# Expert weights loaded in rows of 8 KB instead of 4 KB, one expert to a piece

## The chip, the cores and the metric

The kernel runs on one core of a Trainium2 chip. The metric is the device time of one execution in microseconds (us), the median of several runs. Instructions run on five engines, each with its own queue: TensorE (PE) for matrix products, whose weight loads (PEld) are shown apart; VectorE (DVE); ScalarE (ACT); GpSimd (POOL); and SyncE (SP), which here only issues DMA transfers. The transfers of a core share 16 DMA engines.

## The reference

One encoder layer over 256 tokens of width 1024 in float32. Two mixing branches (stick-breaking attention and retention) are gated, added and projected; after that comes a mixture of experts, which is the stage that this case is about:

```python
def hierarchical_moe(xn, ...):               # xn: 256 tokens x 1024
    group_probs = softmax(xt @ w_group_router + b_group_router)
    p_group, g_sel = top_k(group_probs, 1)                  # 1 of 4 groups
    top_vals, top_idx = top_k(in_group_expert_logits, 2)    # 2 of its 4 experts
    gate = softmax(top_vals) * p_group
    ...
    for e in range(16):
        hidden = silu(xt @ w_exp_gate[e]) * (xt @ w_exp_up[e])   # 1024 -> 512
        y = y + combine[:, e:e + 1] * (hidden @ w_exp_down[e])   # 512 -> 1024
```

The result is added to the layer's stream and normed once more. The weights of the 16 experts are 16 x 3 x 2 MiB = 96 MiB, and every one of them is read.

## The kernel before

**Stages.** The input projections, the two branches and the output projection come first and are not touched. Their weights also come as DMA transfers of 1 MiB, with rows of 1 KB or 2 KB, and one table, `dec`, comes with rows of 8 KB. Then the router picks the experts of each token, and the experts are worked through in eight pairs, `i` = 0 to 7, each expert with up to 64 token places.

**The work on a pair on PE.** `gather` brings the tokens of four pairs to their places with one-hot matrices (32 products of 128x256, line 945, ahead of pair 0 between the first pieces of its gate, and again ahead of pair 4). Its result `xgt` is the stationary operand of `proj` (line 996), which runs once for gate and once for up: eight blocks `c` of 128 input features, each for both experts `j`. The matrix `hn` (the normed stream) is the stationary operand of the gather's products, read through `features(c2, c)`, which says which 128 input features make block `c`: it has to be the set of rows that the weight tile holds at that place. `hidden` (line 1016) transposes the pair's hidden values in four blocks of 128; `down` (line 1032) multiplies them with the down weights; `scatter` (line 1050) adds the pair's result to the tokens. The order on PE for a pair is gate, down of the pair before, up; in the tail it is up of pair 7, down of pair 6, down of pair 7.

**The loads.** All weights go through 25 slots of 8 KB a partition (1 MiB each). `plan` puts the loads down in the order in which they are used: g0, u0, g1, d0, u1, g2, d1, u2, g3, d2, u3, d3, g4, u4, then g, d, u of pairs 5 and 6, then g7, u7, d6, d7 (g, u and d are gate, up and down, each four pieces of 1 MiB, written here g0.0 to g0.3). `pump` (line 163 issues) hands out loads as long as the list of free slots has one; the list is first in, first out. A piece's slot goes back to the list in `after`, which `proj` and `down` call behind the products of a piece, and SP waits in the program for those products before it issues the load that takes the slot. The SP queue is in order: a load that waits holds back all behind it. The transfers of SP count on eight semaphores in turn (DMAHW0 to DMAHW7), so each also waits until the eighth before it has landed.

**A piece before.** For gate and up, piece `r` has features 256r to 256r+255 of both experts of the pair, two consecutive rows of 512 floats to a partition, in two transfers of 512 KB, one for each expert. A down piece has 256 rows of one expert in one transfer, as two rows of 1024 floats a partition that are 128 rows apart. Either way a contiguous run is 4 KB. The work slot, which holds the hidden values and the one-hot matrices of a pair, is taken in `after` when u0.0 is dropped.

Of the kernel before, what the change touches and what calls it, by code (L numbers as in the profile page):

```python
# [17 lines left out]
P = 128  # L18
T = 256
D = 1024  # L20
# [62 lines left out]
def pack(ins):  # L83
    w = np.concatenate([ins["w_group_router"][0], ins["w_expert_router"][0]], axis=1)
    b = np.concatenate([ins["b_group_router"][0], ins["b_expert_router"][0]])
    return np.ascontiguousarray(np.concatenate([
        ins["norm_mix_g"][0].reshape(KC, P).T,
        ins["b_gate"][0].reshape(16, P).T,
        ins["ret_norm_g"][0].reshape(8, P).T,
        ins["norm_ffn_g"][0].reshape(8, P).T,  # L90
        np.broadcast_to(b[None, :], (P, 20)),
        w.reshape(KC, P, 20).transpose(1, 0, 2).reshape(P, 160),
        ins["norm_final_g"].reshape(8, P).T,
        ins["norm_ffn_g"][0].reshape(4, P, 2).transpose(1, 0, 2).reshape(P, 8),
    ], axis=1))


# [1 line left out]
def layer(ctx: ExitStack, tc, cst, dec, prm, x, w_in, w_gate, w_sb_out, w_ret_out,  # L99
          w_out, w_exp_gate, w_exp_up, w_exp_down, out):  # L100
    nc = tc.nc
    pe, act, dve, pool, sp = nc.tensor, nc.scalar, nc.vector, nc.gpsimd, nc.sync
# [17 lines left out]
    def take(shape=(P, 2048), dt=F32):  # L120
        s = free.pop(0)
        uid[0] += 1
        t = big.tile(list(shape), dt, name=f"b{uid[0]}", tag=f"s{s}")
        held[id(t)] = (s, t)
        return t
# [5 lines left out]
    def small(shape, dt=F32, name=None, bufs=1, tag=None):  # L131
        uid[0] += 1
        return sm.tile(list(shape), dt, name=f"{name}_{uid[0]}", tag=tag or name, bufs=bufs)

    def bank(name="d", dt=F32):
        uid[0] += 1
        return pp[name].tile([P, 512 if dt == F32 else 1024], dt, name=f"p{uid[0]}", tag=name)
# [7 lines left out]
    raws = {}  # L145
# [5 lines left out]
    def rows(w, r0, nk, c0, n):  # L151
        return w[r0:r0 + nk * P, c0:c0 + n].rearrange("(kc p) n -> p kc n", p=P)

    def plan(key, shape, parts, hook=None):
        loads.append((key, shape, parts, hook))

    def pump():
        while loads and loaded[0] < limit[0] and free:
            key, shape, parts, hook = loads.pop(0)
            t = raws[key] = take(shape)  # L160
            loaded[0] += 1
            for i, (at, src) in enumerate(parts):
                sp.dma_start(t[at], src)
                if hook:
                    hook(i)
# [6 lines left out]
    def drop(key):  # L172
        give(raws.pop(key))
# [19 lines left out]
    ident = cw[:, 2048 - P:2048]  # L193
# [4 lines left out]
    ident = identr.bitcast(F32)  # L198
# [259 lines left out]

    def plan_rows(which, w, i):
        for r in range(4):  # L460
            e = [w[0, 2 * i + j][256 * r:256 * r + 256].rearrange("(p k) n -> p k n", k=2) for j in range(2)]
            plan((which, i, r), [P, 2, 2, 512], [((slice(None), j), e[j]) for j in range(2)])

    def plan_down(i):
        for r in range(4):
            e = rows(w_exp_down[0, 2 * i + r // 2], 256 * (r % 2), 2, 0, D)
            cut = (i, r) == (NP - 1, 3)
            plan(("d", i, r), [P, 2, D],
                 [((slice(None), k), e[:, k]) for k in range(2)] if cut else [(slice(None), e)])
# [11 lines left out]
    for which, i in STEPS:  # L481
        if which == "d":
            plan_down(i)
        else:
            plan_rows(which, w_exp_gate if which == "g" else w_exp_up, i)
# [3 lines left out]
    key, shape, parts, hook = loads[2]  # L489
# [253 lines left out]
    i = 0  # L743
# [138 lines left out]
    xgt = take([P, KC, T])  # L882
# [50 lines left out]
    y2, work, gs = [], {}, {}  # L933

    def features(c2, c):
        return slice(256 * c2 + c, 256 * c2 + 256, 2)

    def gather(k, pt, cs=range(4)):

        for c2 in cs:  # L940
            ps = bank("m").rearrange("p (c s) -> p c s", c=2)
            for tb in range(NB):
                for h in range(2):
                    for c in range(2):
                        pe.matmul(ps[:, c, :], hn[h][:, tb, features(c2, c)], pt[tb].rearrange("p e s -> p (e s)"),  # L945
                                  start=c == 0 and tb == 0 and h == 0, stop=c == 1 and tb == 1 and h == 1,
                                  skip_group_check=True)
            tt(xgt[:, 2 * c2:2 * c2 + 2, :], ps,
               fp[:, 2 * c2:2 * c2 + 2][:, :, None].to_broadcast([P, 2, 2 * P]), op=ALU.mult)
# [23 lines left out]

    def after(key):
        drop(key)
        if not work and key == ("u", 0, 0):
            w = take([P, 2048])
            work.update(b=w[:, 0:512], ht=[w[:, 512 + 512 * k:1024 + 512 * k].rearrange("p (f s) -> p f s", f=4)
                                           for k in range(2)],
                        pb=w[:, 1536:1664].bitcast(BF16), S=[small([P, T], F32R, "S")])  # L980
        if not y2 and key == ("u", 0, 3):
            w = take([P, 2048], F32R)
            y2.append(w[:, 0:1024].rearrange("p (h n) -> p h n", h=2))
            work["S"].append(w[:, 1024:1024 + T])
        pump()

    def proj(i, which, ps, hook):
        o = 64 * (i % 4)
        for r in range(4):
            if hook:  # L990
                hook(r)
            w = raws[(which, i, r)]
            for k in range(2):
                c = 2 * r + k
                for j in range(2):
                    pe.matmul(ps[64 * j:64 * j + 64, :], xgt[:, c, o:o + 64], w[:, j, k, :],  # L996
                              start=c == 0, stop=c == KC - 1)
            after((which, i, r))

    def gate(i, hook=None):  # L1000
        g = bank("g")
        proj(i, "g", g, hook)
        return g
# [4 lines left out]
    def up(i, hook=None):  # L1008
        u = bank("g")
        proj(i, "u", u, hook)  # L1010
        stt(work["b"], u, gs[i][:, 0:1], work["b"], op0=ALU.mult, op1=ALU.mult)  # L1011

    def hidden(i):
        hps = bank("m").rearrange("p (f s) -> p f s", f=4)
        for f in range(4):
            pe.transpose(hps[:, f, :], work["b"][:, f * P:(f + 1) * P], ident)  # L1016
        act.activation(work["ht"][i % 2], hps, AF.Copy)  # L1017

    def down(i, hook=None):

        ht = work["ht"][i % 2]
        ys = [(bank(b), cs) for b, cs in zip("gm", pieces(i))]
        for r in range(4):
            if hook:
                hook(r)
            w = raws[("d", i, r)]
            j = r // 2
            for y, cs in ys:
                for k in range(2):
                    f = 2 * (r % 2) + k  # L1030
                    for q in range(2):
                        pe.matmul(y[64 * q:64 * q + 64, cs], ht[:, f, 64 * j:64 * j + 64],  # L1032
                                  w[:, k, 512 * q + cs.start:512 * q + cs.stop],
                                  start=r == 0 and k == 0, stop=r == 3 and k == 1)
            after(("d", i, r))
        for y, cs in ys:
            hilo(y2[0][:, 0, cs], y2[0][:, 1, cs], y[:, cs])
# [56 lines left out]
    def head(first):  # L1094
# [21 lines left out]
        for i in range(1, NP):  # L1116
            def in_gate(r):
                if r == 2:
                    tables(i)
                    if i != 4:  # L1120
                        hidden(i - 1)

            def in_up(r):
                if r == 2 and i < NP - 1:
                    scatter(i - 1)
                if r == 2 and i == NP - 1:
                    for q in range(2):
                        final_gain(q)

            if i == 4:  # L1130
                pt = [onehot(1, tb, rank[:, tb, :]) for tb in range(NB)]
                gather(1, pt, [0, 1])
                hidden(3)
                gather(1, pt, [2, 3])
                down(3)
            places(i)
            g = gate(i, in_gate)
            silu(i, g)
            if first and i == 2:
                most.append(nc.values_load(cnt[0:1, 0:1], min_val=0, max_val=T))  # L1140
            if i != 4 and i < NP - 1:
                down(i - 1)
            up(i, in_up)

    def tail():
        i = NP - 1

        def in_first(r):
            if r == 2:
                hidden(i)  # L1150

        def in_second(r):
            if r == 1:
                scatter(i - 1)

        down(i - 1, in_first)
        down(i, in_second)
# [83 lines left out]
```

## Time and profile before

| what | value |
|---|---|
| median of 3 runs | 463.96 us (463.85 to 464.1) |
| profiled execution, its own time | 464.75 us |
| its span, first to last instruction | 463.0 us |
| mean granted TensorE clock | 0.994 |
| PE busy | 443.4 us (96%) |
| DMA | 142.49 MB, mean 308 GB/s |

Shares of busy time are means over the whole span. PE is shown busy nearly throughout, yet a matrix product that waits for its operand can count as busy, so the chain of waits and the DMA rate in each stretch say more. The chain that ended last goes over PE for 80% of the span and over DMA for 14%, all of the latter behind 385 us but for the first microseconds.

### The profile page before, as it was taken

To read this page: it belongs to the slowest core of one execution; us is meant where nothing else is said; L and a number is where in the kernel's file an instruction comes from. 1 tells how busy PE (TensorE), PEld (TensorE's weight loads), DVE (VectorE), ACT (ScalarE), POOL (GpSimd) and SP (SyncE) were. 2 spreads that over 40 slices of the span, in tenths; PEclk is the share of its full clock that TensorE was granted. 3 is DMA by queue.
4 is the path that set the end of the run, shared out by engine and by line. 5 is a ranking of instruction groups with operands and counts; after the bars stand their busy time and mean duration, and the time that the engine had idled before them with its cause. 6 is when DMAs were issued, how large, how long until landed. Compare 5 with 4: busy or idle time off the path is not lost.

```text
span 463.0 us, 6743 instructions
## 1 busy us (share of the span) xinstructions
PE 443.4 (96%) x2715; PEld 298.8 (65%) x2715; DVE 186.9 (40%) x349; ACT 166.7 (36%) x246; POOL 22.2 (5%) x36
## 2 busy tenths in 40 slices
PE   7999999999999999999999999999989999999881
PEld 6699878888899999999996333333353333333240
DVE  4756487654457865578538410101031001010003
ACT  3643688895653655444543020101000010102003
POOL 2400110110002200000001000000000000000000
PEclk9999999999999999999999999999999999999997
DMA  8999975249302279995949999999999999999972
GB/s 282 353 382 392 388 250 172 90 121 316 107 1 92 92 237 372 408 398 183 368 159 335 346 370 390 410 408 411 408 409 410 409 410 409 409 408 409 410 288 97
DMA packets 58037, 142.49 MB, mean 308 GB/s; under 512 B 3344, under 2 KB 23952, under 8 KB 57872
## 3 DMA queue, kind: packets, MB, share of 16 engines
q1 hardware_dynamic: 57568, 141.35, 81.2%
q10 hardware_dynamic: 432, 0.65, 0.5%
q8 instruction: 23, 0.38, 0.3%
q14 instruction: 14, 0.11, 0.1%
HBM read 140.93 MB, written 1.05 MB: 307 GB/s over the span
## 4 chain that ended last, share of the span: by engine, by line
PE 80%; DMA 14%; DVE 2%; ACT 1%; issue 1%; POOL 1%; SPq 0%; ACTq 0%; DVEq 0%
PE p L294 20%; PE p L996 17%; PE p L1032 8%; PE p L281 8%; PE p L284 7%; PE p L282 7%; DMA b<-in_w_exp_down 6%; DMA b<-in_w_exp_up 5%; DMA b<-in_w_exp_gate 2%; PE p L945 2%; PE z L586 1%; PE p L1050 1%; DMA b<-in_x 1%; PE p L688 1%; PE p L629 1%
## 5 line engine op out<-in xcount | busy, mean ns | idle before, releaser
L253 DVE TENSOR_TENSOR b<-b,b 128x1024 fp32r<-128x1024 f32 x72 | 88.7, 1241 | 71.7 <-ACT b L251 70.6
L996 PE MATMUL p<-b,b 128*64 128x512 f32 x512 | 117.1, 597 | 0.2 <-DMA b<-in_w_exp_up 0.2
L294 PE MATMUL p<-b,b 128*128 128x512 f32 (+1 forms) x504 | 102.7, 359 | 0.5 <-ACT b L251 0.3
L251 ACT ACTIVATE b<-b 128x1024 fp32r<-128x1024 f32 x72 | 75.5, 1056 | 76.6 <-PE p L282 47.7
L294 PEld LDWEIGHTS p<-b,b 128*128 128x128 f32 x504 | 82.6, 190 | 14.6 <-ACT b L251 0.7
L996 PEld LDWEIGHTS p<-b,b 128*64 128x64 f32 x512 | 35.8, 137 | 68.1 <-issue 64.4
L281 PE MATMUL p<-b,b 128*128 128x256 f32 x288 | 71.6, 286 | 0.0
L282 PE MATMUL p<-b,b 128*128 128x256 f32 x288 | 70.7, 283 | 0.0
L1032 PE MATMUL p<-b,b 128*64 128x512 f32 (+1 forms) x288 | 57.8, 548 | 2.7 <-DMA b<-in_w_exp_down 1.9
L281 PEld LDWEIGHTS p<-b,b 128*128 128x128 f32 x288 | 55.1, 191 | 0.5
L282 PEld LDWEIGHTS p<-b,b 128*128 128x128 f32 x288 | 55.2, 192 | 0.0
L1032 PEld LDWEIGHTS p<-b,b 128*64 128x64 f32 x288 | 20.2, 137 | 38.5 <-issue 32.3
L284 PE MATMUL p<-b,b 128*128 128x256 f32 x288 | 41.1, 283 | 0.0
L573 DVE SCALAR_TENSOR_TENSOR b<-p,b 128x512 fp32r<-128x512 f32 (+1 forms) x13 | 7.4, 566 | 83.3 <-ACT b L572 83.3
L284 PEld LDWEIGHTS p<-b,b 128*128 128x128 f32 x288 | 37.4, 192 | 0.0
L1011 DVE SCALAR_TENSOR_TENSOR b<-p,share,b 128x512 f32<-128x512 f32 x8 | 6.0, 751 | 62.6 <-PE p L996 62.6
L572 ACT ACTIVATE b<-p 128x512 fp32r<-128x512 f32 (+1 forms) x13 | 6.4, 495 | 53.5 <-PE p L1032 52.9
L972 ACT ACTIVATE b<-p 128x256 fp32r<-128x256 bf16 x4 | 1.5, 386 | 38.1 <-PE p L971 38.1
L972 ACT ACTIVATE S<-p 128x256 fp32r<-128x256 bf16 x4 | 1.5, 384 | 37.4 <-PE p L971 37.4
L1006 ACT ACTIVATE b<-p,share 128x512 f32<-128x512 f32 x8 | 5.5, 688 | 21.3 <-PE p L996 21.3
L1017 ACT ACTIVATE b<-p 128x512 f32<-128x512 f32 x8 | 4.8, 597 | 22.9 <-PE p L1016 22.9
L1188 POOL TENSOR_TENSOR rf<-rf,mhalf 128x1 f32<-128x1 f32 x2 | 1.1, 542 | 208.1 <-DVE rf L1187 208.1
(172 smaller groups left out, 338.2 us busy)
## 6 DMA issues: line engine op xcount, KB each, us to landing
b<-in_w_exp_gate SPq DMA_DIRECT2D x64, 512.0 KB, 10.2
b<-in_w_exp_up SPq DMA_DIRECT2D x64, 512.0 KB, 10.2
b<-in_w_exp_down SPq DMA_DIRECT2D x31, 1024.0 KB, 12.7
b<-in_w_in SPq DMA_DIRECT2D x17, 1024.0 KB, 14.3
b<-in_w_gate SPq DMA_DIRECT2D x8, 1024.0 KB, 5.3
b<-in_w_ret_out SPq DMA_DIRECT2D x4, 1024.0 KB, 5.0
b<-in_w_out SPq DMA_DIRECT2D x4, 1024.0 KB, 11.5
b<-in_w_sb_out SPq DMA_DIRECT2D x2, 1024.0 KB, 9.4
```

The source lines that it names most:

```text
L251: act.activation(hi, raw, AF.Copy)
L253: tt(lo, raw, hi.bitcast(F32), op=ALU.subtract)
L281: pe.matmul(ps, wh[:, k, cs], h[:, k, :], start=k == 0, stop=False)
L282: pe.matmul(ps, wh[:, k, cs], l[:, k, :], start=False, stop=False)
L284: pe.matmul(ps, wl[:, k, cs], h[:, k, :], start=False, stop=k == nk - 1)
L294: pe.matmul(ps[tb], kth(a, k)[:, tb * P:(tb + 1) * P], b[:, j, :], start=n == 0 and k == 0, stop=n == 2 and k == KC - 1)
L572: act.activation(hi, src, AF.Copy)
L573: stt(lo, src, 1.0, hi.bitcast(F32), op0=ALU.mult, op1=ALU.subtract)
L945: pe.matmul(ps[:, c, :], hn[h][:, tb, features(c2, c)], pt[tb].rearrange("p e s -> p (e s)"), start=c == 0 and tb == 0 and h == 0, stop=c ...
L996: pe.matmul(ps[64 * j:64 * j + 64, :], xgt[:, c, o:o + 64], w[:, j, k, :], start=c == 0, stop=c == KC - 1)
L1011: stt(work["b"], u, gs[i][:, 0:1], work["b"], op0=ALU.mult, op1=ALU.mult)
L1032: pe.matmul(y[64 * q:64 * q + 64, cs], ht[:, f, 64 * j:64 * j + 64], w[:, k, 512 * q + cs.start:512 * q + cs.stop], start=r == 0 and k == ...
```

## The change

A gate or up piece now has 512 features of one expert, four consecutive rows (8 KB) to a partition: pieces 0 and 1 are the first 512 features of the two experts, pieces 2 and 3 the second 512. A down piece has the same 256 rows as before, but two consecutive ones to a partition (8 KB). Each piece is one transfer; only the very last down piece is still cut in two, as before, and has rows of 4 KB. `features`, the table of gains that goes with it and the transposes in `hidden` take their columns to match: the step in `hn` goes from 2 to 4 floats (8 to 16 bytes), that in the hidden values from 1 to 2 floats (4 to 8 bytes). `proj` reads the two pieces of a half in turn and drops both behind the second block pair; the work slot is taken when g0.3 is dropped.

```diff
-        ins["norm_ffn_g"][0].reshape(4, P, 2).transpose(1, 0, 2).reshape(P, 8),
+        ins["norm_ffn_g"][0].reshape(2, P, 4).transpose(1, 0, 2).reshape(P, 8),
...
     def plan_rows(which, w, i):
         for r in range(4):
-            e = [w[0, 2 * i + j][256 * r:256 * r + 256].rearrange("(p k) n -> p k n", k=2) for j in range(2)]
-            plan((which, i, r), [P, 2, 2, 512], [((slice(None), j), e[j]) for j in range(2)])
+            e = w[0, 2 * i + r % 2][512 * (r // 2):512 * (r // 2) + 512].rearrange("(p k) n -> p k n", k=4)
+            plan((which, i, r), [P, 4, 512], [(slice(None), e)])
 
     def plan_down(i):
         for r in range(4):
-            e = rows(w_exp_down[0, 2 * i + r // 2], 256 * (r % 2), 2, 0, D)
+            e = w_exp_down[0, 2 * i + r // 2][256 * (r % 2):256 * (r % 2) + 256].rearrange("(p k) n -> p k n", k=2)
...
     def features(c2, c):
-        return slice(256 * c2 + c, 256 * c2 + 256, 2)
+        return slice(512 * (c2 // 2) + 2 * (c2 % 2) + c, 512 * (c2 // 2) + 512, 4)
...
-        if not work and key == ("u", 0, 0):
+        if not work and key == ("g", 0, 3):
             w = take([P, 2048])
...
-            w = raws[(which, i, r)]
+            w = [raws[(which, i, r // 2 * 2 + j)] for j in range(2)]
             for k in range(2):
                 c = 2 * r + k
                 for j in range(2):
-                    pe.matmul(ps[64 * j:64 * j + 64, :], xgt[:, c, o:o + 64], w[:, j, k, :],
+                    pe.matmul(ps[64 * j:64 * j + 64, :], xgt[:, c, o:o + 64], w[j][:, c % 4, :],
                               start=c == 0, stop=c == KC - 1)
-            after((which, i, r))
+            if r % 2:
+                after((which, i, r - 1))
+                after((which, i, r))
...
         for f in range(4):
-            pe.transpose(hps[:, f, :], work["b"][:, f * P:(f + 1) * P], ident)
+            o = 256 * (f // 2) + f % 2
+            pe.transpose(hps[:, f, :], work["b"][:, o:256 * (f // 2) + 256:2], ident)
```

On SP, at the loads g2.2 to u2.1 (the names end in the tensor that is loaded; in brackets stand the semaphores that the issue waits for), before:

```order
L163 DMA b_2524<-in_w_exp_gate 128x1024 [waits DMAHW4_49,PE_49]
L163 DMA b_2524<-in_w_exp_gate 128x1024 [waits DMAHW5_49]
L163 DMA b_2546<-in_w_exp_gate 128x1024 [waits DMAHW6_49,PE_49]
L163 DMA b_2546<-in_w_exp_gate 128x1024 [waits DMAHW7_49]
L163 DMA b_2569<-in_w_exp_down 128x2x1024 [waits DMAHW0_49,PE_49]
L163 DMA b_2580<-in_w_exp_down 128x2x1024 [waits DMAHW1_49,PE_49]
L163 DMA b_2597<-in_w_exp_down 128x2x1024 [waits DMAHW2_49,PE_49]
L163 DMA b_2615<-in_w_exp_down 128x2x1024 [waits DMAHW3_49,PE_49]
L163 DMA b_2630<-in_w_exp_up 128x1024 [waits DMAHW4_49,PE_49]
L163 DMA b_2630<-in_w_exp_up 128x1024 [waits DMAHW5_49]
```

and the same loads of the change:

```order
L163 DMA b_2525<-in_w_exp_gate 128x2048 [waits DMAHW2_49,PE_49]
L163 DMA b_2527<-in_w_exp_gate 128x2048 [waits DMAHW3_49,PE_49]
L163 DMA b_2558<-in_w_exp_down 128x2048 [waits DMAHW4_49,PE_49]
L163 DMA b_2575<-in_w_exp_down 128x2048 [waits DMAHW5_49,PE_49]
L163 DMA b_2577<-in_w_exp_down 128x2048 [waits DMAHW6_49,PE_49]
L163 DMA b_2599<-in_w_exp_down 128x2048 [waits DMAHW7_49,PE_49]
L163 DMA b_2614<-in_w_exp_up 128x2048 [waits DMAHW0_49,PE_49]
L163 DMA b_2616<-in_w_exp_up 128x2048 [waits DMAHW1_49,PE_49]
```

The order of the loads is the same and each still waits for PE to free its slot, but a gate or up piece is one issue instead of two, and the eight semaphores span 8 MiB of gate and up instead of 4 MiB.

On PE, from the last two pieces of g0 to the first half of u0 (L996 is `proj`; the name behind the arrow is the weight tile; L887 adds the stream itself), before:

```order
L996 MATMUL p_2489<-b_1594,b_2418 64x512 x4
L996 MATMUL p_2489<-b_1655,b_2418 64x512 x4
L887 MATMUL p_2435<-b_2084,identr_80 128x512
L887 MATMUL p_2435<-b_2300,identr_80 128x512
L996 MATMUL p_2582<-b_1687,b_2418 64x512 x4
L996 MATMUL p_2582<-b_1690,b_2418 64x512 x4
```

and of the change:

```order
L996 MATMUL p_2471<-b_1592,b_2402 64x512
L996 MATMUL p_2471<-b_1652,b_2402 64x512
L887 MATMUL p_2418<-b_2072,identr_80 128x512
L887 MATMUL p_2418<-b_2286,identr_80 128x512
L996 MATMUL p_2562<-b_1683,b_2402 64x512
L996 MATMUL p_2562<-b_1685,b_2402 64x512
L996 MATMUL p_2562<-b_1683,b_2402 64x512
L996 MATMUL p_2562<-b_1685,b_2402 64x512
```

The products are the same in number, shape and order; they now alternate between two weight tiles, so that neither tile of a half is free before the half's last products.

## Rows read from the trace of the kernel before

**Rows 1.** The page: GB/s in 40 slices of 11.6 us.

```profile
GB/s 282 353 382 392 388 250 172 90 121 316 107 1 92 92 237 372 408 398 183 368 159 335 346 370 390 410 408 411 408 409 410 409 410 409 409 408 409 410 288 97
```

**Rows 2.** The chain that ended last, its end: start us, us, what.

```profile
382.38 2.95 PE p L996 x13
385.34 15.30 DMA b<-in_w_exp_up
...
434.68 15.69 DMA b<-in_w_exp_down
...
450.41 1.52 PE p L1032 x12
```

**Rows 3.** Waits of the SP queue: us in total, times, longest.

```profile
SPq L163 <- DMA b<-in_w_exp_up: 38.8, 45, 1.1
...
SPq L163 <- PE p L996: 26.0, 19, 3.2
```

**Rows 4.** The timeline of SP: start us, us, the loads issued.

```profile
339.30 9.24 SPq L163 DMA_DIRECT2D b<-in_w_exp_gate  x8
...
410.93 9.21 SPq L163 DMA_DIRECT2D b<-in_w_exp_up  x8
```

**Rows 5.** Stretches; the last three columns: clock, DMA share, GB/s.

```profile
36.00:44.00 8.00, 8.00 (x69) 8.00 (x68) 5.24 (x15) 3.17 (x3) 0.00 (x0) 1.00 1.05 387
46.00:48.00 2.00, 2.00 (x11) 1.70 (x11) 1.48 (x2) 0.48 (x1) 0.00 (x0) 1.00 1.03 420
295.00:325.00 30.00, 29.74 (x150) 10.38 (x148) 2.79 (x10) 3.94 (x7) 0.00 (x0) 1.00 1.03 409
270.00:275.00 5.00, 4.87 (x28) 1.79 (x26) 1.14 (x6) 0.98 (x2) 0.00 (x0) 1.00 1.00 392
275.00:280.00 5.00, 5.00 (x26) 1.69 (x24) 0.00 (x0) 0.69 (x1) 0.00 (x0) 1.00 1.03 382
280.00:285.00 5.00, 5.00 (x26) 1.62 (x24) 0.00 (x0) 0.60 (x1) 0.00 (x0) 1.00 0.97 366
```

**Rows 6.** The issue of `dec` on SP.

```profile
36.55 2.58 SPq L163 DMA_DIRECT2D b<-dec  x1
```

**Rows 7.** Single issues on SP, in windows of their own.

```profile
261.36 0.38 SPq L163 DMA_DIRECT2D b<-in_w_exp_down  x1
265.60 0.37 SPq L163 DMA_DIRECT2D b<-in_w_exp_down  x1
271.17 0.34 SPq L163 DMA_DIRECT2D b<-in_w_exp_up  x1
```

**Rows 8.** The chain that ended last, on PE where the pairs begin.

```profile
249.47 2.20 PE p L945 x16
...
253.53 1.16 PE p L945 x8
...
261.98 3.58 PE p L996 x16
265.83 7.02 PE p L996 x32
...
273.90 3.58 PE p L996 x16
```

**Rows 9.** Matrix products at line 284, in the same chain.

```profile
214.35 0.96 PE p L284 x8
```

**Rows 10.** Weight loads by line: busy us, mean ns of one.

```profile
L284 PEld LDWEIGHTS p<-b,b 128*128 128x128 f32 x288 | 37.4, 192 | 0.0
L945 PEld LDWEIGHTS p<-pt,b 128*128 128x128 f32 x64 | 8.1, 195 | 4.4 <-DVE pt L863 2.3 <-issue 1.6 <-DVE b L948 0.5
```

**Rows 11.** The timeline of PE: its first stop for a landing in the tail.

```profile
424.96 1.93 PE L996 MATMUL p<-b,b 128*64 128x512 f32 x6 [0.22 <-DMA b<-in_w_exp_up]
```

**Rows 12.** Waits of PE's weight loads: us in total, times, longest.

```profile
PEld p L1032 <- DMA b<-in_w_exp_down: 3.9, 4, 1.5
PEld p L996 <- DMA b<-in_w_exp_up: 2.6, 5, 1.1
```

## The prediction

> **What bounds the kernel now.** I read the page's rate of DMA by slice first [rows 1]. From about 290 us to the last load it stands at 408 to 410 GB/s without a break, while the slices from 231 to 290 us lie between 159 and 390. So the experts' stage has two parts: one in which loads do not come at the full rate, and one in which they do. The chain that ended last then says which engine the end hangs on [rows 2]: up to 385.34 us it goes over PE, from there to 450.4 over loads, and behind the last landing stand 1.52 us of `down` and the closing work to 463.0, together 12.6 us that the change does not touch. SP's waits say what holds the loads [rows 3]: 38.8 us for landings of up loads alone (the eight semaphores in turn: the queue is full, nothing is lost), but also 26.0 us for products of `proj`, that is for a slot to come free. The question is where the last loss of the second kind is, since all that follows it moves at the DMA rate.
>
> The slots are handed out first in, first out, so it can be followed in the code which load takes whose slot: d1.0 that of g0.2, d1.1 that of g0.3, (the work slot is u0.0's), d1.2 that of u0.1, d1.3 that of u0.2, u2.0 to u2.3 those of g1.0 to g1.3, g3 those of d0, d2 those of u1. The issues agree with PE's chain: d1.1 goes out at 261.36, d1.2 at 265.60, u2.0 at 271.17 [rows 7]; u0's first half ends at 261.98 + 3.58 = 265.56, and g1.0 is done three quarters into the 7.02 us from 265.83 (u0.2, u0.3, g1.0, g1.1), at 271.1 [rows 8].
>
> Now for each late issue I add what is still to be moved at the full rate, and look for the latest end. The full rate: 28 pieces of 1 MiB (g5 to g7 in the order of the loads) lie between 339.30 and 410.93 us [rows 4], 2.558 us each, 409.9 GB/s. From u2.0 on there are 68 pieces: 271.17 + 68 x 2.558 = 445.1. For d1.2, 70 pieces: 265.60 + 179.1 = 444.7. For d1.1, 71: 261.36 + 181.6 = 443.0. So u2.0's slot decides. The last load lands at 450.37 [rows 2], 5.3 us behind 445.1: the way from issue to landing, and dips between 270 and 285 us, worth (18 + 28 + 44) x 5 / 410 = 1.1 us [rows 5]. I carry the 5.3 over unchanged.
>
> **Rows of 8 KB.** Before has just one load of them, `dec`, issued at 36.55 us [rows 6]. From 46 to 48 us, when it is moved, DMA runs at 420 GB/s; in the 2 KB rows ahead (36 to 44 us) at 387, in the 4 KB rows of the experts at 409 [rows 5]. A second way, without `dec`: one of 16 engines spends 2048 x 16 / 387 = 84.7 ns on a row of 2 KB and 4096 x 16 / 409.9 = 159.9 on one of 4 KB. The second 2 KB cost 75.2, so some 9.5 ns are spent on each row whatever its length, and a row of 8 KB takes 159.9 + 2 x 75.2 = 310.3 ns, 422 GB/s. The two agree. I take 421 GB/s, 2.49 us a piece. Bounds: 2.48 (422), and 2.558 should long runs of 8 KB be no faster than 4 KB; the short stretch of `dec` (128 rows) is the weak point of this term. The saved second issue of a gate or up piece is worth nothing, since SP has time to spare (it sits waiting for landings), and the deeper queue of 8 MiB too, as 4 MiB already kept DMA full.
>
> **Slots in pairs.** The two pieces of a half are dropped together, so that of gate and up pieces 0 and 2 come free one piece (1.8 us) later. The work slot now is g0.3's, so d1.1 waits for u0.0 and with it for the first half of u0: 265.6 instead of 261.36, together with d1.2. u2.0 and u2.1 go out at 272.85, u2.2 and u2.3 at 273.90 + 3.58 = 277.5 [rows 8]. At 2.49 us a piece, d1.1 and d1.2 fill the time to 270.6; d1.3 (u0.2 and u0.3 done, 265.83 + 3.51 = 269.3) is in time and fills it to 273.1; u2.0 and u2.1 are in time by 0.2 us and fill it to 278.0; u2.2 by 0.5 us; g3 takes slots of `down`, which still come one by one from 279 us on. So the last loss moves from u2.0 to d1.1: 265.6 + 71 x 2.49 = 442.4, against 445.1, a gain of 2.7 us. With 2.48 it is 441.7, a gain of 3.4; with 2.558 it is 447.2, a loss of 2.1. The pairs alone thus cost 2.1, and the longer rows give back 71 x 0.068 = 4.8.
>
> **Wider steps in the stationary operand.** The gather now reads `hn` in steps of 16 bytes. No row shows that step. The nearest: at 8 bytes the gather's weight loads take 195 ns, at 4 bytes those of line 284, same shape, 192 [rows 10]; and eight products of the gather take 1.16 us [rows 8] where eight at line 284 take 0.96 [rows 9], while sixteen take 2.20: 17 to 25 ns more for one. I take another 17 ns for the wider step, x 32 = 0.5 us, which shifts all slots above. Bounds: nothing, and a weight load twice as long that nothing hides, 195 x 32 = 6.2 us. The second gather (ahead of pair 4) pays the same, but then the loads are ahead of nothing and PE has room. The transposes of `hidden`, with steps of 8 bytes, cost 4 x 3 ns a pair by the same rows, which I leave out.
>
> The Trainium skill, page "SBUF — State Buffer", section "Door 1: The DMA port swizzle", says that SBUF is read in lines of 16 bytes, and that full speed wants at least two hits in a line. By that rule a step of 8 bytes (two floats to a line) is still free, and one of 16 bytes (one float) is not. It speaks against this change; the size of the penalty is not given, so by the rule the sum is open upwards, to the rival below.
>
> **The tail on PE.** If loads land 2.2 us earlier, PE has to be there earlier. It runs without a stop until 424.74 us, when it first waits for up of pair 7 [rows 11], and then its weight loads wait for landings for 3.9 + 2.6 = 6.5 us [rows 12], in part under products that still run; about 4.7 of it is time that PE can give back. In pairs, u7's second half cannot start before u7.3 has landed, so that it ends one piece later behind that landing; but the eight `down` pieces that follow take PE some 1.8 us each, as the pieces of `proj` do (7.02 / 4, [rows 8]), and DMA 2.5, and the lag is made up by d6.3. The end stays the last landing + 12.6 us. Infinitely fast loads would gain about 4.7.
>
> **Sum.** -2.7 + 0.5 = -2.2 us. The profiled execution takes 464.75 by its own time (span 463.0); the median of the runs is 463.96, 0.8 below. I take the shift from the median: 461.8 us. A change of 0.2%, 0.9 us, is what can be told from none here.
>
> **Rivals.**
> - *The longer rows pay in full, and the dips go too.* 422 GB/s, a free gather, no dips: -3.4 - 1.1 = -4.5, at PE's limit: 459.5. For it: a queue twice as deep when slots do come. Against it: the dips are shown with DMA nearly fully busy (share 0.97 to 1.03), so they need not be the queue.
> - *It cancels.* Break-even of rows and pairs lies at (445.1 - 0.5 - 265.6) / 71 = 2.521 us a piece, 416 GB/s. `dec`'s 420 is only 1% away, from 2 us of trace. Then 463 to 465.
> - *Slower, since a row of 8 KB is no faster.* The pairs' 2.1 and the gather's 0.5 remain: 466.6. Against it stand both ways of working out the row; for it, that no slice of the page is above 410 GB/s [rows 1].
> - *Slower, since the gather's weight loads stall.* PE's frees shift by what the 32 products lose, and the gain of 2.7 is gone at 84 ns each; at 150 ns it is +2.1, 466.1, and the second gather takes the same from PE's room in the tail. This is the case of the page's rule. Against it: the step from 4 to 8 bytes cost little, and a weight load runs beside the product before it.
>
> **How the numbers follow.** Forecast 461.8 (own range 460.6 to 462.9) 0.50; the full gain 0.12; cancelling 0.16; rows no faster 0.11; the stalled gather 0.11. Faster by over 0.2%: 0.62; slower by over 0.2%: 0.22; between: 0.16. The range of 459.6 to 465.6 takes in the first three and the milder part of both slower ones.
>
> **What would show it.** Right: in the stretch from 295 to 325 us DMA at 418 to 423 GB/s; d1.1 and d1.2 issued together at about 266 us and no gap in DMA behind them; the last landing at about 448. The gather's products at 137 to 160 ns each show the term of the step. Wrong: a rate of 409 to 412 (the row), a first gather longer by over 2 us (the step), or gaps in DMA at u2.0 to g3 although PE keeps its times (the slots). A PE that stops for pairs of pieces before pair 7 would show that I misjudged the room in the tail.

## The result, and the profile after

The changed kernel takes 466.06 us (median of 5 runs, 465.86 to 466.9), the kernel before 463.96 (5 runs, 463.29 to 464.1): a ratio of 1.0051, interval 1.0038 to 1.0064, so 2.1 us slower, where 2.2 us faster was forecast. The profiled execution takes 466.04 us, near its median, while that of before lay 0.8 above its own; so the spans, 463.0 and 464.2, differ by only 1.2.

The loads did what was forecast. Here are the page's rates by slice of the changed kernel:

```profile
GB/s 280 353 383 391 390 263 162 86 140 322 75 3 90 92 260 383 421 385 186 359 152 305 211 344 385 428 418 424 419 422 423 419 423 419 421 423 418 422 280 96
```

and one stretch of it (last three columns: clock, DMA share, GB/s):

```profile
295.00:325.00 30.00, 29.74 (x148) 10.60 (x146) 3.94 (x13) 3.25 (x6) 0.00 (x0) 1.00 1.01 422
```

422 GB/s stands against 409 [rows 5]: rows of 8 KB are worth 3%, and keep it to the end. Yet the slices from 243 to 290 us are lower than before (305, 211, 344, 385 against 335, 346, 370, 390, [rows 1], slices being 11.6 us in both). What holds the loads back there, and PE all the way, shows in the chain that ended last (start us, us, what), which now goes over PE for 92% of the span:

```profile
249.01 4.01 PE p L945 x16
253.02 1.87 PE p L996 x8
254.89 2.09 PE p L945 x8
256.97 1.87 PE p L996 x8
258.84 2.08 PE p L945 x8
...
265.17 3.58 PE p L996 x16
...
343.33 4.15 PE p L945 x16
347.48 0.85 PE p L1019 x4
348.33 3.98 PE p L945 x16
...
447.84 5.33 PE p L1035 x48
453.17 1.37 PE p L1053 x14
```

Sixteen products of the gather take 4.01 us, not 2.20, and eight take 2.09, not 1.16 [rows 8]. The first gather's 32 products lose 4.01 + 2.09 + 2.08 - (2.20 + 1.16 + 1.17) = 3.65 us, 114 ns each, the second's 3.7 more. `down` of the tail (L1035) stands in the chain without a wait for a landing, where before the end hung on one [rows 2]. The weight loads by line (busy us, mean ns of one) say what is slow:

```profile
L945 PEld LDWEIGHTS p<-pt,b 128*128 128x128 f32 x64 | 15.4, 330 | 4.3 <-DVE pt L863 2.3 <-issue 1.6 <-DVE b L948 0.3
L1019 PEld LDWEIGHTS p<-identr,b 128*128 128x128 f32 x32 | 4.7, 209 | 2.6 <-DVE share L965 1.8 <-issue 0.8
```

A weight load of the gather takes 330 ns instead of 195 [rows 10], 135 more, of which 114 come out in the time of a product. L1019 is the transposes of `hidden`.

The loads alone would have allowed a slightly earlier end. The last one is issued at 433.6 us and lands 17.4 us later:

```profile
L163 SPq DMA_DIRECT2D b<-in_w_exp_down x1: 328/328/328, 433.6 to 433.6; - x1
DMA to landing us min/median/max: 17.4/17.4/17.4
```

So it lands at 451.0, and with the 1.52 us of `down` behind a last landing [rows 2] the scatter (L1053) could begin at 452.5. PE reaches it at 453.17, 0.6 us later.

### The profile page after: what moved, and what is told of

The parts are those of the page before. It is cut to its first block, busy times and chain, and to the rows that moved or that the text cites. A ratio compares the mean times of both kernels' runs of the same rounds, so it can differ in the third digit from the quotient of the medians.

```text
span 464.2 us, 6673 instructions
## 1 busy us (share of the span) xinstructions
PE 447.6 (96%) x2715; PEld 305.8 (66%) x2715; DVE 186.7 (40%) x349; ACT 166.8 (36%) x246; POOL 22.1 (5%) x36
## 4 chain that ended last, share of the span: by engine, by line
PE 92%; DVE 2%; DMA 1%; ACT 1%; issue 1%; POOL 1%; SPq 0%; ACTq 0%; DVEq 0%
PE p L996 24%; PE p L294 19%; PE p L1035 12%; PE p L281 8%; PE p L284 7%; PE p L282 7%; PE p L945 4%; PE p L1053 2%; PE z L586 1%; PE p L1019 1%; DMA b<-in_x 1%; PE p L688 1%; PE p L629 1%; PE z L617 1%; PE p L831 1%
## 5 line engine op out<-in xcount | busy, mean ns | idle before, releaser
L996 PE MATMUL p<-b,b 128*64 128x512 f32 x512 | 115.1, 596 | 0.0
L996 PEld LDWEIGHTS p<-b,b 128*64 128x64 f32 x512 | 35.1, 137 | 66.3 <-issue 64.6
L1035 PE MATMUL p<-b,b 128*64 128x512 f32 (+1 forms) x288 | 56.7, 546 | 0.0
L1035 PEld LDWEIGHTS p<-b,b 128*64 128x64 f32 x288 | 20.4, 137 | 34.0 <-issue 31.2
L945 PEld LDWEIGHTS p<-pt,b 128*128 128x128 f32 x64 | 15.4, 330 | 4.3 <-DVE pt L863 2.3
L945 PE MATMUL p<-pt,b 128*128 128x256 f32 x64 | 16.5, 414 | 1.3 <-DVE pt L863 1.2
## 6 DMA issues: line engine op xcount, KB each, us to landing
b<-in_w_out SPq DMA_DIRECT2D x4, 1024.0 KB, 11.6
```

## The experiments

Each ran beside the kernel before on the same chip; ratios, and differences in us, are to that. The kernel before took 464.2 to 464.6 us there, up to 0.7 more than in the result above, so a time that was forecast in absolute terms can be off by as much; the intervals reach 0.6 to 0.8 us to either side. Theory A: the wide step in the gather makes the change slower. Theory B: slots that come free in pairs do.

**The wide step alone**, with the loads of before:

```diff
-        return slice(256 * c2 + c, 256 * c2 + 256, 2)
+        return slice(512 * (c2 // 2) + 2 * (c2 % 2) + c, 512 * (c2 // 2) + 512, 4)
```

> The loads of the kernel before (4 KB rows, slots freed one by one), and the gather alone reads its stationary operand in steps of 16 bytes; the blocks of features then no longer match the rows of the weights, so this part of the computation is changed, with the same amount of work. Theory A (the wide step doubles the gather's weight loads, and these make the change slower): the first gather's products take 4.0 + 2.1 + 2.1 us as in the changed kernel, not 2.2 + 1.2 + 1.2, slots come free 3.6 to 3.7 us later from the first gate on, and since the rows of 4 KB set the end here, the time is 463.96 + 3.6 = 467.6 us (466.8 to 468.2). Theory B (slots freed in pairs make the change slower, the step costs little): 464.0 to 464.6.

Measured: 468.23 us, ratio 1.0084 (1.0069 to 1.0100), 3.9 us more. Theory A, at the upper edge of its range; B's ends at 464.6. The first sixteen products on PE's timeline:

```profile
249.10 4.01 PE L945 MATMUL p<-pt,b 128*128 128x256 f32 x16
```

The chain that ended last goes over PE up to the last issue at 436.85 us; the load issued there ends it, 2.8 us later than in [rows 2]:

```profile
437.47 15.70 DMA b<-in_w_exp_down
453.21 1.51 PE p L1032 x12
```

**The change without the step:**

```diff
-        return slice(512 * (c2 // 2) + 2 * (c2 % 2) + c, 512 * (c2 // 2) + 512, 4)
+        return slice(256 * c2 + c, 256 * c2 + 256, 2)
```

> The changed kernel, with the gather reading in steps of 8 bytes as before, so that the blocks of features do not match the rows of the weights (this part of the computation is changed, with the same amount of work). Theory A: the prediction's sum without the step's term: 463.96 - 2.7 = 461.3 us (460.5 to 462.2), DMA at 421 GB/s, PE again waiting for landings in the tail, the first gather 2.2 us. Theory B: still 465 to 466, with gaps in DMA behind 260 us.

Measured: 461.85 us, ratio 0.9954 (0.9940 to 0.9967), 2.1 us less than before. Theory A again; B falls. The prediction's accounting of the slots can be read here, in SP's timeline: d1.1 and d1.2 go out together at 265.02.

```profile
265.02 0.80 SPq L163 DMA_DIRECT2D b<-in_w_exp_down  x2
```

From there, 71 pieces at 2.49 us make 441.8, and with the 5.3 us carried over 447.1; the last piece has landed at 446.7, by the chain that ended last, here with the first gather ahead:

```profile
248.91 2.20 PE p L945 x16
...
429.30 17.37 DMA b<-in_w_exp_down
446.71 1.52 PE p L1035 x12
448.23 1.37 PE p L1053 x14
```

**The stream stored by twos.** The features that fit the 8 KB rows, in another order of columns in `hn`, so that the gather's step is 8 bytes:

```diff
+    def quads(t, q, tb, part=None):
+        v = t[:, tb, 512 * q:512 * q + 512].rearrange("t (a p b) -> t p a b", a=2, b=2)
+        return v if part is None else v[:, 64 * part:64 * part + 64]
...
-        hi, v = hn[0][:, tb, wo_cols[n]], xt[:, tb, wo_cols[n]]
+        hi, v = quads(hn[0], n // 2, tb, n % 2), xt[:, tb, wo_cols[n]].rearrange("t (p a b) -> t p a b", a=2, b=2)
...
```

> The changed kernel, with the normed stream stored in another order of its columns (in runs of two floats), so that the gather reads the features that fit the 8 KB rows in steps of 8 bytes; the writes of the stream go out, and the eight products that add it are read, in runs of 8 bytes. Theory A: as the change without the wide step, plus what the other order costs the writes and these eight products, at most 1 us: 461.3 to 462.3 us. Theory B: 465 to 466.

Measured: 462.38 us, ratio 0.9958 (0.9944 to 0.9972), 1.9 us less than before, and the features now match the rows. Theory A, at the upper edge of its range. The eight products that add the stream take 527 ns instead of 429 by the mean, 0.8 us in all; by the medians this kernel takes 0.5 us more than the change without the step. What the writes in the other order cost was not measured.

**Pairs alone**, meant to show the price of slots freed by twos with rows of 4 KB:

```diff
-        if not work and key == ("u", 0, 0):
+        if not work and key == ("g", 0, 3):
...
-            after((which, i, r))
+            if r % 2:
+                after((which, i, r - 1))
+                after((which, i, r))
```

> The kernel before with its own rows of 4 KB and its own gather, but with the slots of gate and up pieces freed two by two and the work slot taken one piece earlier, as in the change. The prediction's term for it is +2.1 us: 466.0 (465.5 to 466.5) by theory A and B alike; theory B, which puts the whole loss of the change here, needs at least +2.1 + 4.8 = 6.9, for the faster rows are then to be made up as well: 470 or more. Nothing (464.0) would say that the last loss of DMA time is not where the prediction put it.

Measured: 465.26 us, ratio 1.0020 (1.0007 to 1.0033), 0.9 us more: a miss, and of the experiment, not only of the number. SP waits for the products that read the piece, not for the place in the program where its slot is given back, and here each piece is still read by one block pair alone. So only the work slot moved. That shows: d1.1 now waits for u0.0 and goes out at 263.11, u2.0 at 270.39, when g1.0 is done (three quarters into the 7.02 us below, 270.3) and not g1.1 (272.1). The pairs' price was therefore not tested by itself.

```profile
263.11 0.38 SPq L163 DMA_DIRECT2D b<-in_w_exp_down  x1
...
270.39 0.34 SPq L163 DMA_DIRECT2D b<-in_w_exp_up  x1
```

```profile
265.05 7.02 PE p L996 x32
```

By the accounting, 263.11 + 71 x 2.558 = 444.7 now decides over 270.39 + 68 x 2.558 = 444.3, which would decide in this trace with the work slot as before: 0.4 us, where 0.9 was measured (0.3 to 1.5).

**The down rows alone:**

```diff
-            e = rows(w_exp_down[0, 2 * i + r // 2], 256 * (r % 2), 2, 0, D)
+            e = w_exp_down[0, 2 * i + r // 2][256 * (r % 2):256 * (r % 2) + 256].rearrange("(p k) n -> p k n", k=2)
...
-            pe.transpose(hps[:, f, :], work["b"][:, f * P:(f + 1) * P], ident)
+            o = 256 * (f // 2) + f % 2
+            pe.transpose(hps[:, f, :], work["b"][:, o:256 * (f // 2) + 256:2], ident)
```

> The kernel before with only its down pieces in rows of 8 KB (and the transposes of the hidden values in steps of 8 bytes to match); gate, up, slots and gather as before. By the prediction's accounting u2.0's slot decides as before, and of the 68 pieces behind it 24 are down pieces: 24 x 0.07 = 1.7 us less, 462.3 us (461.8 to 462.9). If a rate gained in part of the loads is lost again elsewhere: 463.9.

Measured: 463.3 us, ratio 0.9965 (0.9948 to 0.9983), 1.6 us less than before, as the accounting has it (1.7). The time itself lies above the range expected, since the kernel before took 464.64 us beside it.

**The step in one gather only**, first the second gather, then the first (from the changed kernel; `k` is 0 in the first gather, 1 in the second; shown is the first of the two runs, the other has `k == 1`). Theory A1: the step hurts only through the slots that the first gather holds back. Theory A2: it also makes PE itself the bound.

```diff
-                        pe.matmul(ps[:, c, :], hn[h][:, tb, features(c2, c)], ...
+                        pe.matmul(ps[:, c, :], hn[h][:, tb, slice(256 * c2 + c, 256 * c2 + 256, 2) if k == 0 else features(c2, c)], ...
```

> The changed kernel with the wide step only in the gather ahead of pair 4; the first reads in steps of 8 bytes, so that its blocks do not match the weights' rows (that part of the computation is changed, with the same amount of work). If the step hurts only by holding back the slots at the start (theory A1): as without the step, 461.8 us. If it also hurts since PE itself becomes the bound (theory A2): PE has lost 3.7 us here and 0.7 in the transposes, of about 4.7 to 5 us that it has left, so that it is late by next to nothing against the kernel before: 463.2 to 463.9.

Measured: 462.91 us, ratio 0.9965 (0.9952 to 0.9979), 1.6 us less than before. The time lies between the two theories (461.8, and 463.2 to 463.9), and with the kernel before at 464.64 us beside it, the difference does not decide either.

> The changed kernel with the wide step only in the first gather; that ahead of pair 4 reads in steps of 8 bytes, so that its blocks do not match the weights' rows (that part of the computation is changed, with the same amount of work). By theory A1: as the changed kernel, 466.0 us. By theory A2: slots 3.6 us later, -2.1 + 3.6 = +1.5 against the kernel before by the loads, and less than that by PE: 465.0 to 465.6.

Measured: 466.22 us, ratio 1.0033 (1.0020 to 1.0046), 1.5 us more than before. That is A2's difference, but A1's, 2.1 as in the changed kernel, lies at the edge of the interval. What decides is the two chains that ended last, of the kernel with the step in the second gather and of the one with it in the first, each with its start and its end:

```profile
249.54 2.20 PE p L945 x16
...
444.61 5.33 PE p L1035 x48
449.94 1.38 PE p L1053 x14
```

```profile
249.69 4.10 PE p L945 x16
...
434.12 17.36 DMA b<-in_w_exp_down
451.52 1.51 PE p L1035 x12
453.04 1.38 PE p L1053 x12
```

With the step in the second gather PE ends the chain without a wait, as A2 has it: L1053 begins 200.4 us behind the first gather's start. Without the step at all a landing ends it, and L1053 begins 199.3 behind that start, 1.1 less. With the step in the first, the loads end it, since all slots came some 3.6 us later, and L1053 begins 203.4 behind. With both, in the changed kernel, it is 204.2 (453.17 - 249.01), and PE gets there by itself.

**Pairs 0 and 1 in pieces of both experts.** The stream stored by twos, and 8 KB rows, except that gate and up of the first two pairs come as every other 4 KB of the same rows, both experts to a piece:

```diff
+            if i < 2:
+                e = [w[0, 2 * i + j][512 * (r // 2):512 * (r // 2) + 512].rearrange("(p a k) n -> p a k n", a=2, k=2)[:, r % 2]
+                     for j in range(2)]
+                plan((which, i, r), [P, 2, 2, 512], [((slice(None), j), e[j]) for j in range(2)])
+                continue
...
-        if not work and key == ("g", 0, 3):
+        if not work and key == ("u", 0, 0):
```

> The kernel with the stream stored by twos and 8 KB rows, but with gate and up of pairs 0 and 1 in pieces of both experts with runs of 4 KB (every other run of the same rows), freed one by one, and the work slot at u0.0 as before. By the prediction's accounting the last loss is again at u2.0's slot, and 68 pieces at 2.49 instead of 2.558 us follow: 4.6 us less, of which PE can follow about 4: 459.8 to 460.6 us. If slots in pairs cost nothing, as the kernel with the stream stored by twos, 462 us.

Measured: 460.23 us, ratio 0.9911 (0.9898 to 0.9923), 4.1 us less than before and some 2.2 less than with the pairs (two differences measured on different chips, each known to about 0.6); the fastest of all kernels here. PE is nearly at its limit: the chain that ended last has products of `down` at its end, and no landing between them; the weight loads of `down` still wait 1.2 us for landings.

```profile
441.30 4.20 PE p L1049 x36
445.54 1.52 PE p L1049 x12
447.06 1.38 PE p L1067 x14
```

**Four steps side by side**, in the kernel before, each part of a gather from a line of its own:

```diff
...
+                        if c2 == 0:
+                            pe.matmul(at[0], x[:, 128 * c:128 * c + 128], at[1], **how)
+                        elif c2 == 1:
+                            pe.matmul(at[0], x[:, c:256:2], at[1], **how)
+                        elif c2 == 2:
+                            pe.matmul(at[0], x[:, c:384:3], at[1], **how)
+                        else:
+                            pe.matmul(at[0], x[:, c:1024:8], at[1], **how)
```

> The kernel before with its four parts of a gather read in steps of 1, 2, 3 and 8 floats (4, 8, 12 and 32 bytes), each from a line of its own, so that the blocks do not match the weights' rows (that part of the computation is changed, with the same amount of work). If what counts is how many reads fall in one line of 16 bytes: 1 and 2 floats alike (weight loads of 192 to 195 ns), 8 floats as 4 in the changed kernel (332), 3 floats between or as 8. If the time grows with the distance: 8 floats far above 332, some 600. One look, for the rows of the weight loads; the time is of no interest.

One run (465.76 us). The weight loads by line (count, then ns min/median/max), for steps of 4, 8, 12 and 32 bytes:

```profile
L950 PEld LDWEIGHTS p<-pt,b x16: 186/188/192, 249.4 to 342.0; 128*128 128x128 f32 x16
...
L952 PEld LDWEIGHTS p<-pt,b x16: 193/196/199, 250.3 to 342.9; 128*128 128x128 f32 x16
...
L954 PEld LDWEIGHTS p<-pt,b x16: 253/261/266, 253.4 to 345.3; 128*128 128x128 f32 x16
...
L956 PEld LDWEIGHTS p<-pt,b x16: 312/340/345, 256.8 to 347.2; 128*128 128x128 f32 x16
```

188, 196, 261, and 340 ns at 32 bytes, where the changed kernel has 332 (median) at 16. Nearly all of the price begins between 8 and 12 bytes, and from 16 to 32 it hardly grows. The rule that the prediction weighed (the Trainium skill, page "SBUF — State Buffer", section "Door 1: The DMA port swizzle") wants at least two reads in a line of 16 bytes for full speed and puts a penalty on each read that goes to a new line. These rows agree with it: two floats to a line are all but free, and one float to a line costs about the same at 16 bytes as at 32. The transposes in the last section do not fit it.

## Why the prediction was wrong

- **Rows of 8 KB: right.** 422 GB/s, as worked out from the cost of a row (421 was taken). The short stretch of `dec` was a good witness after all.
- **Slots in pairs: borne out.** In the change without the step the last landing was 0.4 us from the sum, and the gain 2.1 us (1.5 to 2.8), where the sum without the step says 2.7. Giving the pairs up for two pairs of experts alone brought some 2.2 us, where the accounting has 265.6 + 71 x 2.49 against 271.17 + 68 x 2.49, 1.9 us. The pairs' price by itself was never measured.
- **The wider step: the step of the sum that failed.** It was sized at 17 ns a product, 0.5 us a gather, by drawing on what the step from 4 to 8 bytes had cost. It measured 114 ns, 3.65 us a gather, seven times as much, though inside the bounds given (nothing to 6.2 us). The rival "the gather's weight loads stall" had the mechanism (slots later by what the products lose, and PE's room in the tail taken by the second gather), and 114 ns is beyond its 84 ns at which the gain is gone. Its price by the slots alone falls short, though: -2.7 + 3.65 makes 0.95 us more than before, where 2.1 was measured; 0.6 of the rest is PE's own lateness at the end, and 0.6 that the gain without the step measured 2.1. The rival was given 11% since the step from 4 to 8 bytes cost little. But that row could not speak against the Trainium skill's rule: by the rule that step is free and the next is not.
- **"PE has room" at the second gather: wrong with that size.** The two gathers took 3.65 + 3.7 us of PE, and the transposes of `hidden` 0.74 - 0.65 us a pair (in the chains of the changed kernel and of that before), 0.7 in all: 8.1 us. PE's waits for landings in the tail were 6.5 us [rows 12], and they are used up; the 1.2 us by which the span grew is close to 8.1 - 6.5 less the 0.46 us by which the gather began earlier. So nearly all of the 6.5 us could be given back, not the 4.7 that the prediction took. In the changed kernel two bounds stand close together: slots that come 3.65 us late, and, 0.6 us behind them, PE itself.
- **The transposes** were put at 3 ns a product and cost some 20; off the path in the kernels that end on a load.
- **The dips** from 270 to 285 us stayed with the deeper queue (367, 382 and 359 GB/s in the three stretches of [rows 5]), and for the most part also where the step was away (365, 369, 426); that rival's 1.1 us was not there. The kernel with two pairs as before reached its 4.1 us otherwise.

Two small differences are within what the runs can tell: the gain without the step, 2.1 us against a sum of 2.7 (the interval reaches 2.8), and the work slot's price, 0.9 against 0.4 (0.3 to 1.5).

## What to carry to other kernels

A layout that suits the loads also sets the step at which some engine reads the other operand: follow it to every reader, and look there at the step in bytes. When a price has a threshold by a rule, a cheap row on the near side of it says nothing of the far side; the term has to be kept at its upper bound, or tried by itself. And where transfers wait for slots, adding "issue time plus all that follows at the full rate" for each late issue points to the one that sets the end, here within 0.4 us in the change without the step, and tells which pieces are worth freeing sooner.

## What the hardware showed besides

- The transposes of `hidden`, which are not in the gather's rounded format, pay at 8 bytes already: 209 ns a weight load against 140 at 4 bytes (L1019 above; L1016 in the kernel before), though two floats still fall in each 16 bytes. The same step in the kernel with the down rows alone gives 207. That these are transposes, or that their numbers are unrounded, may be the reason; no run separates the two:

```profile
L1016 PEld LDWEIGHTS p<-identr,b 128*128 128x128 f32 x32 | 3.4, 140 | 2.7 <-DVE share L965 1.8 <-issue 0.8
```

- In the changed kernel the granted clock fell during the second gather, after a stop of PE of about 1 us and 2 us of the gather's slow products (the third column from the right is the clock: 1.00 is 2.4 GHz, 0.50 is 1.2 GHz):

```profile
345.00:346.00 1.00, 1.00 (x6) 1.00 (x6) 0.47 (x1) 0.00 (x0) 0.00 (x0) 0.85 1.02 426
346.00:347.00 1.00, 1.00 (x6) 1.00 (x5) 0.22 (x1) 0.00 (x0) 0.00 (x0) 0.50 1.06 442
347.00:348.00 1.00, 1.00 (x7) 0.93 (x5) 0.49 (x1) 0.00 (x0) 0.00 (x0) 0.50 0.97 401
```

Sixteen products of the gather took 4.15 and 3.98 us about the fall, and 4.01 in the first gather, where the clock stood at 1.00. So the slow weight loads hardly hang on TensorE's clock. It cost the four transposes between the halves 0.1 us (0.85 us in the chain, 0.74 elsewhere). In the kernel with the step in the second gather alone, the same stop and the same slow products passed with the clock at 1.00, so what made it fall is not shown.
